# One segment of the modulation vector, computed by GpSimd during the mixers

## The chip, the cores and the metric

The kernel runs on one core of a Trainium2 chip. The core has TensorE (PE, matrix products into PSUM), VectorE (DVE), ScalarE (ACT), GpSimd (POOL) and SyncE (SP, which issues the weight loads here); all but SyncE's queue work on tiles in SBUF. The metric is the device time of one execution in microseconds (us); less is better.

## What is computed

Two transformer blocks on 256 tokens of width 2048, all in float32. The first block begins with a modulation vector of six segments of 2048 values from the condition `c`:

```python
c_act = jax.nn.silu(c)
mod = c_act @ ada_w[l] + ada_b[l]
sh1, sc1, g1, sh2, sc2, g2 = jnp.split(mod, 6, axis=-1)
h = rmsnorm(x, norm1_g[l]) * (1.0 + sc1[:, None]) + sh1[:, None]
x = x + g1[:, None] * token_mixer(h, ...)
h = rmsnorm(x, norm2_g[l]) * (1.0 + sc2[:, None]) + sh2[:, None]
x = x + g2[:, None] * moe_ffn(h, ...)
```

`ada_w` is 2048 x 12288. Segment 5 is `g2`, the factor behind the experts. `token_mixer` projects `h` to queries, keys and values, runs four kinds of attention (mixers) and projects their outputs with `w_out`. The second block (a long convolution, a gating unit, a feed-forward layer) takes no part of the modulation.

## The kernel before

A float32 product is made of three products of a split operand (`mm3`, L155): each weight tile that arrives in SBUF (`wraw`) is copied by ScalarE into a high part (`whi`, L146), VectorE takes the remainder (`wlo`, L149), and TensorE runs `hi*hi`, `lo*hi`, `hi*lo` (L158 to L160). There are five `wraw` buffers and three pairs of `whi` and `wlo`. One chunk is 256 rows by 512 columns of a weight, 512 KB.

The stages follow each other: `phase0` (the filters of the second block, segments 0 and 1 of the modulation, the first projections, to about 200 us), `mixers` (the other projections, the attentions and `w_out`, to about 620 us), the router, the experts (`moe`), then `block2`. All that the change touches runs in `mixers`.

A segment of the modulation is computed in four blocks of 512 columns, each in four steps (`ada_steps`, L456). A step loads two pieces of `ada_w`, 256 rows by 512 columns each (L467), so four row tiles of 128, and multiplies each row tile by its 128 values of `silu(c)`. There are two ways to do that. On TensorE (L473) four matmuls with 32 equal columns of `silu(c)` add up in one bank of PSUM; after the last step VectorE copies the bank to `arow` (L488), TensorE transposes it (L491), and VectorE sums the parts and adds the bias. On VectorE (`dve`) the first row tile is multiplied by its value of `silu(c)` per partition (L475), each other one is multiplied and added to `arow` in one instruction (L477), and at the end four matmuls with a column of ones sum over the partitions (L485). `ADA_DVE` lists the blocks that take the second way: blocks 1 and 3 of segments 2, 4, 3 and 5.

Steps of the segments run between other work: `rest` (L609) yields step by step in the order of segments 2, 4, 3, 5; every chunk of a projection adds 0.5 to an account and every softmax batch 0.7 (`hook`), and a step is written whenever the account reaches 1. What is left is written behind `w_out`. Pieces go to seven buffers in turn (`ada_place`: four named `a`, three `a2`); a load waits until its buffer has been read.

Every engine works in order through its own instructions. Their order is set by a scheduler in the framework, from the order in which the code is written, priorities and its own cost estimates, so an edit can move instructions on every engine. A softmax batch (`softmax_batch`) is a chain: TensorE's scores (L820), VectorE's sum with the bias (L837) and maximum (L839), ScalarE's exponential (L845), TensorE's transposes (L850), VectorE's copy (L852), TensorE's product with the values (L857). The mixers have 30 batches, 12 of them in the first attention stage (`nsa`), which also begins with a chain of small steps (L933 to L992).

Of the kernel before, what the change touches and what calls it, by code (L numbers as in the profile page):

```python
# [9 lines left out]
F32 = mybir.dt.float32  # L10
# [3 lines left out]
OP = mybir.AluOpType  # L14
# [4 lines left out]
P = 128  # L19
# [6 lines left out]
DFF = 5632  # L26
KF = DFF // P
HOOK_GEMM, HOOK_ATT = 0.5, 0.7
ADA_DVE = [(s, b) for s in (2,4,3,5) for b in (1,3)]

PAD = 16
TINY = float(np.finfo(np.float32).tiny)
# [107 lines left out]
class Body:  # L140
# [312 lines left out]
            return self.wp.tile([P, 2, 512], F32, name="wraw", tag="wraw", bufs=self.nraw)  # L453
        return self.piece([P, 2, 512], t)

    def ada_steps(self, seg, b, dve=False):  # L456


        nc, w = self.nc, self.i["ada_w"][0]
        c0 = seg * D + b * 512  # L460
        sb = self.awp.tile([P, 512], F32, name="arow", tag="arow", bufs=1)
        ps = None if dve else self.bank("ada")
        for q in range(4):
            for h in range(2):
                k0 = 4 * q + 2 * h
                raw = self.ada_place()
                self.last_ada = nc.sync.dma_start(raw, w[k0 * P:(k0 + 2) * P, c0:c0 + 512]  # L467
                                                  .rearrange("(k p) n -> p k n", p=P))
                for j in range(2):
                    k, r = k0 + j, raw[:, j]  # L470
                    if not dve:
                        m = 32 * (2 * h + j)
                        nc.tensor.matmul(ps[m:m + 32], self.cact[:, k], r, start=q == 0, stop=q == 3)  # L473
                    elif k == 0:
                        nc.vector.tensor_scalar(sb, r, self.cs[:, k:k + 1], None, OP.mult)  # L475
                    else:
                        nc.vector.scalar_tensor_tensor(sb, r, self.cs[:, k:k + 1], sb, OP.mult, OP.add)  # L477
            if q < 3:
                yield
        n = seg * 16 + b * 4  # L480
        bias, mod = self.v["ada_b"][:, n:n + 4], self.mod[:, seg, b * 4:b * 4 + 4]
        pt = self.bank("ada")
        if dve:
            for a in range(4):
                nc.tensor.matmul(pt[:, a:a + 1], sb[:, a * P:(a + 1) * P], self.ones[:, 0:1], start=True, stop=True)  # L485
            nc.vector.tensor_tensor(mod, pt[:, :4], bias, OP.add)
        else:
            nc.vector.tensor_copy(sb, ps)  # L488
            pt = pt.rearrange("p (a q) -> p a q", a=4)
            for a in range(4):  # L490
                nc.tensor.transpose(pt[:, a], sb[:, a * P:(a + 1) * P], self.ident)  # L491
            s = self.tmp.tile([P, 4], F32, name="adas", tag="modg", bufs=2)
            nc.vector.tensor_reduce(s, pt.rearrange("p a (j r) -> p a r j", r=32)[:, :, 0], AX.X, OP.add)
            nc.vector.tensor_tensor(mod, s, bias, OP.add)
        yield


    def bias_tables(self):
# [104 lines left out]
    def mixers(self):  # L603
        nc, tc, i = self.nc, self.tc, self.i
# [2 lines left out]
        xs = lambda k: (hh[:, k], hl[:, k])  # L607

        def rest():  # L609
            for seg in (2, 4, 3, 5):  # L610
                for b in range(4):
                    yield from self.ada_steps(seg, b, (seg, b) in ADA_DVE)
        bg, last = rest(), self.last_ada
        due = [0.0]

# [7 lines left out]
        with ExitStack() as c0:  # L623
# [9 lines left out]
            def project(col, tag, perm=False, mul=None):  # L633
                t = self.piece([P, 4, S], "k") if tag == "k" else qk(tag, tag)
                for m, p in enumerate(self.gemm(w, KD, col, 512, xs, C4, hook, perm)):
                    take(t[:, m], p, mul)
                return t
# [28 lines left out]
            q, k = project(0, "q", mul=scale), project(512, "k")  # L666
# [3 lines left out]
            q, k = project(2304, "q", mul=scale), project(2816, "k")  # L670
# [31 lines left out]
            acc = self.new_acc()  # L702
# [5 lines left out]
            for g in range(4):  # L708
# [4 lines left out]
                for m in range(4):  # L713
                    k = g * 4 + m
# [28 lines left out]
            r = v[:, 2:4]  # L743
# [5 lines left out]
            t = self.rt.tile([P, 2, 4], F32, name="gnorm")  # L749
# [891 lines left out]
```

## Time and profile before

| what | us |
|---|---|
| median of three runs (lowest, highest) | 2642.29 (2641.45, 2646.45) |
| the profiled execution | 2653.08 |
| its span | 2651.0 |

| engine | busy us | share of the span |
|---|---|---|
| TensorE, matmul | 2578.2 | 97% |
| TensorE, weight load | 2263.1 | 85% |
| VectorE | 1788.8 | 67% |
| ScalarE | 1333.8 | 50% |
| GpSimd | 7.2 | 0% |

All rows come from the profiled execution, which is 10.8 us above the median. Matmuls overlap, and the profile models their ends: a burst of them is priced by the distance between starts. Busy time of other engines is that of each instruction by itself. A row of waits names the engine that waited, its instruction, whom it waited for, then the total in us, how many times and the longest. PEclk is the granted clock of TensorE as a share of full speed (2.4 GHz), DMA the mean busy share of the 16 DMA engines, GB/s what they moved. "SPq" is SyncE's queue, which issues the loads.

### The profile page before, as it was taken

The numbers are of one execution on the slowest core, as the hardware profiler recorded it, in microseconds if no ns is written. First come the engines' busy times: TensorE is split into PE (matmuls) and PEld (weight loads), VectorE is DVE, ScalarE is ACT, GpSimd is POOL, SyncE is SP. The second block draws the span as 40 slices with busy tenths as digits, with TensorE's granted clock in tenths as the row PEclk, the third lists the DMA queues.
The fourth block names the chain that finished last, engine by engine and source line by source line (L and its number), as shares of the span: only waits on it lengthen the run. The fifth ranks groups of instructions, "written<-read, shape, count | busy, mean of one in ns | idle before, by whom it ended". The sixth has DMA issues, their size and how long they took to land.

```text
span 2651.0 us, 43628 instructions
## 1 busy us (share of the span) xinstructions
PE 2578.2 (97%) x17355; PEld 2263.1 (85%) x17355; DVE 1788.8 (67%) x2513; ACT 1333.8 (50%) x1774; POOL 7.2 (0%) x20
## 2 busy tenths in 40 slices
PE   6998999998999999999999999999999999999997
PEld 2476888888788878787998899999999999998886
DVE  4647777777889898988787655555655555555444
ACT  2333444545777777776444444444544444443443
POOL 0000000000000000000000000000000000000000
PEclk7998999998999999999999999999999999999999
DMA  9898799893899999997554555555555556556664
GB/s 358 288 299 292 258 328 323 301 311 115 297 334 326 330 334 376 344 367 281 176 167 128 182 184 184 188 185 186 184 188 190 187 189 190 187 189 199 191 195 138
DMA packets 320394, 640.81 MB, mean 242 GB/s; under 512 B 21748, under 2 KB 36116, under 8 KB 319416
## 3 DMA queue, kind: packets, MB, share of 16 engines
q1 hardware_dynamic: 310768, 618.83, 69.0%
q10 hardware_dynamic: 8392, 13.89, 1.6%
q0 software_dynamic: 1024, 5.25, 0.6%
q8 instruction: 137, 2.24, 0.3%
q14 instruction: 73, 0.60, 0.1%
HBM read 631.02 MB, written 6.35 MB: 240 GB/s over the span
## 4 chain that ended last, share of the span: by engine, by line
PE 72%; DVE 2%; ACT 1%; issue 1%; DMA 0%; ACTq 0%; DVEq 0%
PE ps_y L159 18%; PE ps_y L158 18%; PE ps_y L160 18%; PE ps_u L159 2%; PE ps_g L159 2%; PE ps_g L158 2%; PE ps_u L160 2%; PE ps_u L158 2%; PE ps_g L160 2%; DVE wlo L149 1%; PE ps_b L158 0%; PE ps_b L160 0%; PE ps_b L159 0%; DMA ws<-in_sgu_w_s_dram 0%; ACT whi L146 0%
## 5 line engine op out<-in xcount | busy, mean ns | idle before, releaser
L149 DVE TENSOR_TENSOR wlo<-wraw,whi 128x1024 fp32r<-128x1024 f32 (+1 forms) x972 | 1162.8, 1204 | 651.4 <-ACT whi L146 631.9
L146 ACT ACTIVATE whi<-wraw 128x1024 fp32r<-128x1024 f32 (+1 forms) x972 | 1011.1, 1044 | 933.5 <-PE ps_y L159 457.9
L158 PE MATMUL ps_y<-hH,whi 128*128 128x256 f32 x2432 | 681.5, 280 | 0.0
L160 PE MATMUL ps_y<-hH,wlo 128*128 128x256 f32 x2432 | 679.9, 280 | 0.0
L159 PE MATMUL ps_y<-hL,whi 128*128 128x256 f32 x2432 | 678.6, 279 | 0.0
L158 PEld LDWEIGHTS ps_y<-hH,whi 128*128 128x128 f32 x2432 | 456.8, 188 | 1.9 <-issue 1.7
L160 PEld LDWEIGHTS ps_y<-hH,wlo 128*128 128x128 f32 x2432 | 456.7, 188 | 1.7 <-issue 1.3
L159 PEld LDWEIGHTS ps_y<-hL,whi 128*128 128x128 f32 x2432 | 456.2, 188 | 1.8 <-issue 1.7
L158 PE MATMUL ps_mm<-hH,whi 128*128 128x256 f32 (+1 forms) x784 | 227.2, 290 | 4.4 <-ACT whi L146 4.4
L160 PE MATMUL ps_mm<-hH,wlo 128*128 128x256 f32 (+1 forms) x784 | 226.6, 291 | 2.1 <-DVE wlo L149 2.0
L159 PE MATMUL ps_mm<-hL,whi 128*128 128x256 f32 (+1 forms) x784 | 224.8, 287 | 0.0
L158 PEld LDWEIGHTS ps_mm<-hH,whi 128*128 128x128 f32 (+1 forms) x784 | 149.9, 191 | 25.1 <-issue 12.0
L160 PEld LDWEIGHTS ps_mm<-hH,wlo 128*128 128x128 f32 (+1 forms) x784 | 148.4, 190 | 10.7 <-DVE wlo L149 5.2
L159 PEld LDWEIGHTS ps_mm<-hL,whi 128*128 128x128 f32 (+1 forms) x784 | 148.4, 189 | 1.2 <-issue 0.6
L159 PE MATMUL ps_y<-wlo,actH 128*128 128x512 f32 x352 | 137.2, 390 | 0.0
L160 PE MATMUL ps_y<-whi,actL 128*128 128x512 f32 x352 | 137.1, 389 | 0.0
L158 PE MATMUL ps_y<-whi,actH 128*128 128x512 f32 x352 | 137.0, 390 | 0.0
L159 PE MATMUL ps_y<-wlo,piece 128*128 128x512 f32 x256 | 101.9, 398 | 0.2
L160 PE MATMUL ps_y<-whi,piece 128*128 128x512 f32 x256 | 100.5, 393 | 0.3 <-DVE piece L149 0.3
L158 PE MATMUL ps_y<-whi,piece 128*128 128x512 f32 x256 | 92.0, 394 | 0.7 <-ACT piece L146 0.7
L473 PE MATMUL ps_ada<-piece,cact 128*32 128x512 f32 x488 | 90.1, 655 | 2.5 <-DMA piece<-in_ada_w_dram 1.7
L477 DVE SCALAR_TENSOR_TENSOR arow<-piece,cs,arow 128x512 f32<-128x512 f32 x120 | 89.3, 744 | 1.9 <-DMA piece<-in_ada_w_dram 0.9
(521 smaller groups left out, 3898.5 us busy)
## 6 DMA issues: line engine op xcount, KB each, us to landing
wraw<-in_w_in_dram SPq DMA_DIRECT2D x224, 512.0 KB, 4.1
piece<-in_ada_w_dram SPq DMA_DIRECT2D x186, 512.0 KB, 6.8
wraw<-in_w_ffn_in_dram SPq DMA_DIRECT2D x176, 512.0 KB, 4.5
wraw<-in_exp_w_down_dram SPq DMA_DIRECT2D x125, 512.0 KB, 5.5
wraw<-in_exp_w_up_dram SPq DMA_DIRECT2D x124, 512.0 KB, 5.6
wraw<-in_exp_w_gate_dram SPq DMA_DIRECT2D x122, 512.0 KB, 5.4
wraw<-in_w_ffn_out_dram SPq DMA_DIRECT2D x88, 512.0 KB, 3.7
wraw<-in_w_out_dram SPq DMA_DIRECT2D x64, 512.0 KB, 4.9
```

What stands on the lines that cost most here:

```text
L146: self.nc.scalar.activation(dst, src, AF.Copy)
L149: self.nc.vector.tensor_tensor(dst, src, h.bitcast(F32), OP.subtract)
L158: mm(ps, a[0], b[0], start=start, stop=False)
L159: mm(ps, a[0], b[1], start=False, stop=False)
L160: mm(ps, a[1], b[0], start=False, stop=stop)
L473: nc.tensor.matmul(ps[m:m + 32], self.cact[:, k], r, start=q == 0, stop=q == 3)
L477: nc.vector.scalar_tensor_tensor(sb, r, self.cs[:, k:k + 1], sb, OP.mult, OP.add)
```

## The change

All four blocks of segment 5 go to GpSimd. GpSimd has no instruction in this kernel that multiplies and adds at once, so each row tile but a block's first is multiplied in place (the piece is written over) and then added to an accumulator of its own, `prow`: 64 products and 60 sums. The end of a block is that of the VectorE way, four matmuls with ones. The steps of segment 5 no longer come last: after every three steps of segments 2, 4 and 3 one of segment 5 is written, and the account counts it as a step, so there are 64 steps as before. Line numbers behind the edits rise by 1 to 16.

```diff
--- before.py
+++ after.py
@@ -26,7 +26,7 @@
 DFF = 5632
 KF = DFF // P
 HOOK_GEMM, HOOK_ATT = 0.5, 0.7
-ADA_DVE = [(s, b) for s in (2,4,3,5) for b in (1,3)]
+ADA_DVE = [(s, b) for s in (2, 4, 3) for b in (1, 3)]
 
 PAD = 16
 TINY = float(np.finfo(np.float32).tiny)
@@ -453,12 +453,13 @@
             return self.wp.tile([P, 2, 512], F32, name="wraw", tag="wraw", bufs=self.nraw)
         return self.piece([P, 2, 512], t)
 
-    def ada_steps(self, seg, b, dve=False):
+    def ada_steps(self, seg, b, dve=None):
 
 
         nc, w = self.nc, self.i["ada_w"][0]
         c0 = seg * D + b * 512
-        sb = self.awp.tile([P, 512], F32, name="arow", tag="arow", bufs=1)
+        tag = "prow" if dve is self.nc.gpsimd else "arow"
+        sb = self.awp.tile([P, 512], F32, name=tag, tag=tag, bufs=1)
         ps = None if dve else self.bank("ada")
         for q in range(4):
             for h in range(2):
@@ -472,9 +473,9 @@
                         m = 32 * (2 * h + j)
                         nc.tensor.matmul(ps[m:m + 32], self.cact[:, k], r, start=q == 0, stop=q == 3)
                     elif k == 0:
-                        nc.vector.tensor_scalar(sb, r, self.cs[:, k:k + 1], None, OP.mult)
+                        dve.tensor_scalar(sb, r, self.cs[:, k:k + 1], None, OP.mult)
                     else:
-                        nc.vector.scalar_tensor_tensor(sb, r, self.cs[:, k:k + 1], sb, OP.mult, OP.add)
+                        self.add_product(dve, sb, r, self.cs[:, k:k + 1])
             if q < 3:
                 yield
         n = seg * 16 + b * 4
@@ -493,6 +494,14 @@
             nc.vector.tensor_reduce(s, pt.rearrange("p a (j r) -> p a r j", r=32)[:, :, 0], AX.X, OP.add)
             nc.vector.tensor_tensor(mod, s, bias, OP.add)
         yield
+
+    def add_product(self, engine, acc, t, c):
+
+        if engine is self.nc.vector:
+            engine.scalar_tensor_tensor(acc, t, c, acc, OP.mult, OP.add)
+            return
+        engine.tensor_scalar(t, t, c, None, OP.mult)
+        engine.tensor_tensor(acc, acc, t, OP.add)
 
 
     def bias_tables(self):
@@ -607,9 +616,16 @@
         xs = lambda k: (hh[:, k], hl[:, k])
 
         def rest():
-            for seg in (2, 4, 3, 5):
-                for b in range(4):
-                    yield from self.ada_steps(seg, b, (seg, b) in ADA_DVE)
+
+            far = (x for b in range(4) for x in self.ada_steps(5, b, nc.gpsimd))
+            for n, _ in enumerate(x for seg in (2, 4, 3) for b in range(4)
+                                  for x in self.ada_steps(seg, b, nc.vector if (seg, b) in ADA_DVE else None)):
+                yield
+                if n % 3 == 2:
+                    next(far, None)
+                    yield
+            for _ in far:
+                yield
         bg, last = rest(), self.last_ada
         due = [0.0]
 
```

What the built program shows, at the three places that matter most. First GpSimd, in whose list nothing stood between the fills of the first attention stage (`cs`) and the load of the router's overflow count (`ovi`). Before:

```order
L294 MEMSET gap 128x8
L975 MEMSET cs 128x128 x2
L1333 TENSOR_LOAD ovi
L1334 COMPARE_AND_BRANCH
L1334 UNCONDITIONAL_BRANCH x2
```

Now:

```order
L294 MEMSET gap 128x8
L991 MEMSET cs 128x128 x2
L476 ISA
L476 TENSOR_SCALAR prow<-piece,cs 128x512
L503 TENSOR_SCALAR piece<-piece,cs 128x512
L504 TENSOR_TENSOR prow<-prow,piece 128x512
L503 TENSOR_SCALAR piece<-piece,cs 128x512 x2
L504 TENSOR_TENSOR prow<-prow,piece 128x512 x2
```

One block is one product into `prow` and then 15 pairs of a product and a sum; four such blocks stand in a row.

Second the queue of loads on SyncE, from the loads of the compression weights (`nsa_cmp`) at the start of the first attention stage. Before:

```order
L929 DMA wraw<-in_nsa_cmp_w_k_dram 128x8x128 x2
L929 DMA wraw<-in_nsa_cmp_w_v_dram 128x8x128 x2
L467 DMA piece<-in_ada_w_dram 128x2x512 x16
L191 DMA wraw<-in_w_in_dram 128x2x512
L467 DMA piece<-in_ada_w_dram 128x2x512 x2
```

Now:

```order
L945 DMA wraw<-in_nsa_cmp_w_k_dram 128x8x128 x2
L945 DMA wraw<-in_nsa_cmp_w_v_dram 128x8x128 x2
L468 DMA piece<-in_ada_w_dram 128x2x512 x9
L191 DMA wraw<-in_w_in_dram 128x2x512
L468 DMA piece<-in_ada_w_dram 128x2x512 x5
```

The next weight of a projection stood behind sixteen pieces and stands behind nine.

Third TensorE a little later, from the scores of the compressed keys (`kc`, `q`) to the first softmax batch. Before:

```order
L978 MATMUL ps_b<-kc,q 128x15 x8
L485 MATMUL ps_ada<-vec,arow 128x1 x4
L473 MATMUL ps_ada<-piece,cact 32x512 x5
L992 MATMUL ps_b<-vec,cs 128x128
L820 MATMUL ps_b<-piece,q 128x256 x4
L473 MATMUL ps_ada<-piece,cact 32x512 x9
L850 MATMUL ps_b<-vec,s 128x128 x4
```

Now:

```order
L994 MATMUL ps_b<-kc,q 128x15 x8
L158 MATMUL ps_mm<-hH,whi 128x256
L159 MATMUL ps_mm<-hL,whi 128x256
L158 MATMUL ps_mm<-hH,whi 128x256
L159 MATMUL ps_mm<-hL,whi 128x256
L160 MATMUL ps_mm<-hH,wlo 128x256
L158 MATMUL ps_mm<-hH,whi 128x256
L1008 MATMUL ps_b<-vec,cs 128x128
L836 MATMUL ps_b<-piece,q 128x256 x4
```

Ahead of the transpose of the compressed weights (L992, now L1008) stood nine matmuls of the modulation; now six plain products of the next projection stand there, and 18 more follow behind the scores.

## Rows read from the trace of the kernel before

**Rows 1.** The page: what the DMA queues moved by slice; the chain that ended last.
```profile
GB/s 358 288 299 292 258 328 323 301 311 115 297 334 326 330 334 376 344 367 281 176 167 128 182 184 184 188 185 186 184 188 190 187 189 190 187 189 199 191 195 138
...
PE 72%; DVE 2%; ACT 1%; issue 1%; DMA 0%; ACTq 0%; DVEq 0%
```

**Rows 2.** Busy time by stretch: start:end us, length, busy us (x instructions) by engine, clock, DMA.
```profile
200.00:300.00 100.00, 92.23 (x692) 73.35 (x691) 72.51 (x136) 37.71 (x88) 0.00 (x0) 0.88 0.75 267
300.00:400.00 100.00, 99.21 (x707) 82.14 (x706) 71.73 (x115) 47.20 (x93) 0.00 (x0) 1.00 0.92 319
400.00:500.00 100.00, 99.92 (x712) 82.97 (x710) 68.80 (x109) 46.75 (x89) 0.00 (x0) 1.00 0.90 306
500.00:600.00 100.00, 98.84 (x811) 90.44 (x807) 83.41 (x160) 48.58 (x93) 0.00 (x0) 1.00 0.92 320
```

**Rows 3.** Waits of TensorE, 200 to 590 us: who waited for whom, total us, times, longest.
```profile
PE ps_b L937 <- DVE four L935: 2.3, 2, 1.8
PE ps_ada L485 <- DVE arow L477: 2.1, 2, 1.8
PE ps_b L850 <- ACT s L845: 1.4, 3, 1.1
```

**Rows 4.** Timeline of TensorE, 308 us: start, length us, engine, instruction.
```profile
308.14 0.28 PE L160 MATMUL ps_mm<-hH,wlo 128*128 128x256 f32 x1
308.35 1.07 PE L473 MATMUL ps_ada<-piece,cact 128*32 128x512 f32 x8
309.35 0.38 PE L158 MATMUL ps_mm<-hH,whi 128*128 128x256 f32 x1
309.57 0.28 PE L159 MATMUL ps_mm<-hL,whi 128*128 128x256 f32 x1
```

**Rows 5.** The same view at 317 and at 577 us.
```profile
317.17 0.28 PE L159 MATMUL ps_mm<-hL,whi 128*128 128x256 f32 x1
317.29 0.60 PE L491 MATMUL ps_ada<-vec,arow 128*128 128x128 f32 x4
317.64 0.36 PE L160 MATMUL ps_mm<-hH,wlo 128*128 128x256 f32 x1
...
576.59 0.28 PE L158 MATMUL ps_mm<-hH,whi 128*128 128x256 f32 x1
576.77 1.02 PE L485 MATMUL ps_ada<-vec,arow 128*128 128x1 f32 x8
577.66 0.37 PE L159 MATMUL ps_mm<-hL,whi 128*128 128x256 f32 x1
```

**Rows 6.** VectorE by form, 200 to 590 us: shape, count, busy us, mean ns, idle before.
```profile
L149 DVE TENSOR_TENSOR wlo<-wraw,whi 128x1024 fp32r<-128x1024 f32 x77 | 93.6, 1219 | 31.7 <-ACT whi L146 28.3 <-PE ps_ada L473 3.2
L477 DVE SCALAR_TENSOR_TENSOR arow<-piece,cs,arow 128x512 f32<-128x512 f32 x120 | 89.3, 744 | 1.9 <-DMA piece<-in_ada_w_dram 0.9
...
L488 DVE COPY arow<-ps_ada 128x512 f32<-128x512 f32 x8 | 5.5, 690 | 11.7 <-PE ps_ada L473 11.7
...
L475 DVE TENSOR_SCALAR arow<-piece,cs 128x512 f32<-128x512 f32 x8 | 3.8, 478 | 0.1
```

**Rows 7.** ScalarE by form, 200 to 590 us.
```profile
L146 ACT ACTIVATE whi<-wraw 128x1024 fp32r<-128x1024 f32 x77 | 81.1, 1057 | 125.5 <-PE ps_mm L159 48.4 <-issue 45.2 <-PE ps_mm L160 19.5
```

**Rows 8.** GpSimd by form, whole span.
```profile
L975 POOL MEMSET cs<- 128x128 f32 x2 | 0.3, 204 | 142.8 <-DVE fK L593 142.8
L294 POOL MEMSET gap<- 128x8 f32 x2 | 0.2, 104 | 394.0 <-PE ps_y L160 393.8 <-POOLq L1629 0.3
```

**Rows 9.** Timeline of TensorE in the first attention stage.
```profile
221.66 3.62 PE L473 MATMUL ps_ada<-piece,cact 128*32 128x512 f32 x10 [0.25 <-DVE mod L486]
...
225.21 0.48 PE L992 MATMUL ps_b<-vec,cs 128*128 128x128 f32 x1
```

**Rows 10.** Waits of the DMA queue on SyncE, 200 to 600 us.
```profile
SPq L467 <- PE ps_ada L473: 81.5, 27, 9.0
SPq L467 <- DVE arow L477: 60.4, 34, 7.3
```

## Prediction

> **What bounds the kernel now.** Start with the chain of waits: 72% of the chain that ended last lies on TensorE and 2% on VectorE [rows 1], so time is won by taking work off TensorE or by closing its gaps. All that the change touches lies in the mixers, about 200 to 590 us, so read the busy time by stretch next. From 300 to 600 us TensorE is busy 99.2, 99.9 and 98.8 us of each 100 at a granted clock of 1.00, the 2.4 GHz level. From 200 to 300 us it is busy 92.2 us at a mean of 0.88 [rows 2]. Its idle time over these 400 us is 7.8 + 0.8 + 0.1 + 1.2 = 9.8 us. The list of its waits shows for whom: VectorE or ScalarE, a microsecond or two at a time [rows 3]. VectorE is busy 72.5, 71.7, 68.8 and 83.4 us of each 100 [rows 2], a second engine with a quarter of its time free. ScalarE's waits say how far the weights are split ahead: before the copies into `whi` it sat idle 48.4 + 19.5 us until TensorE had released a buffer [rows 7], so TensorE, not the split, sets the pace. GpSimd does nothing here (the column of x0) [rows 2].
>
> A busy TensorE hides what an instruction costs, since matmuls overlap. The price is the spacing of starts in the timeline. Plain 256-column products start 0.12 us apart. Around one burst of four segment matmuls (eight records) the starts are 308.14 and 309.35, then 309.57 [rows 4]: 1.21 - 0.12 = 1.09 us, and 0.10 us lost in the next, wider spacing. So 1.19 us a burst.
>
> **The change part by part.** Segment 5 (`g2`) has four blocks of 512 columns. Before, blocks 0 and 2 are on TensorE and 1 and 3 on VectorE.
> - TensorE loses two blocks of four bursts: 8 x 1.19 = 9.5 us. It loses their transposes: 317.17 to 317.64 less 0.12, and 0.10 for the next spacing, is 0.45 us [rows 5], twice 0.9. It gains two blocks of the other kind, four 1-column matmuls each: 576.59 to 577.66 less 0.12 plus 0.10 is 1.05 us [rows 5], twice 2.1. Net 9.5 + 0.9 - 2.1 = 8.3 us off the engine that sets the pace.
> - VectorE loses two blocks of one product and 15 product-sums: 2 x (0.478 + 15 x 0.744) = 23.3 us, and two copies of 0.690 us [rows 6]: 24.7 us. The loss is off the path, and worth nothing but room.
> - GpSimd gains 64 products and 60 sums of 128x512. No row has such an operation. The nearest are its own fills: 204 ns for 128 elements and 104 ns for 8 [rows 8], or 0.83 ns an element and 0.10 us fixed. One pass over 512 is then 0.5 us, which as a lower bound gives 124 x 0.5 = 62 us. The upper bound counts a pass for each operand, two for a product (0.95 us) and three for a sum (1.4 us): 145 us. I take the middle, 104 us or 0.84 us an operation, as nothing stands nearer either end. A step of four row tiles is 6.7 us (4 to 9), and 16 steps in 390 us come every 24 us, so GpSimd keeps up and its own time is covered.
> - The four row matmuls of a GpSimd block wait for its last sum, and behind them, in order, stand all matmuls. In the built program at least 78 plain products, 9 us, lie between that sum and them. With a step of 4 to 9 us I price this wait at 0; if that cover went, each would cost up to 9 us, 36 in all.
> - Loads: the same pieces and bytes, a quarter of them for GpSimd, from the same seven buffers. A step takes two, so a buffer comes round after 3.5 steps, at 6.1 us a step 21 us; GpSimd holds its pair for 9 us at most. SyncE's queue already waits 81.5 us for TensorE and 60.4 us for VectorE to free pieces [rows 10] without TensorE idling, so 0.
> - The order of the first attention stage moves. Before, sixteen pieces go ahead of the next weight, and ten records of segment matmuls stand from 221.66 us until the transpose at 225.21 [rows 9]: 3.6 us in a chain of small dependent steps. Now nine go ahead, and plain products stand there instead, which themselves wait for the weight tenth in the queue. That could win 3.6 us or lose as much; I take 0 and keep both ends.
> - Segments 2, 4 and 3 finish later. The last is needed by the router's shift after the last projection, and its row matmuls still stand ahead of 246 plain products of that projection: 0.
> - The hidden term: VectorE and GpSimd side by side. No run shows both at work. If they don't meet, it is 0. If VectorE is stretched in proportion to GpSimd's time, 104 of 390 us or 27%, TensorE's present 9.8 us of idle time, mostly waits for VectorE, grows by 2.6 us. The upper end is in the second rival.
>
> Sum: -8.3 + 2.6 = -5.7 us. The profiled execution took 2653.1 us (span 2651.0), so 2647.4; the median of the runs lies 10.8 us under it, so **2636.6 us**.
>
> The Trainium skill, "SBUF — State Buffer", section "SBUF: two separate sides", says more than proportion: VectorE and GpSimd share one pair of ports as an exclusive lock, and a VectorE operation with two SBUF inputs and a GpSimd operation fully block each other. No run here shows it so far. The remainder `wlo` and the product-sums are of that kind, so it speaks against this change. "GPSIMD Engine Reference", section 3.1, has 4497 ns for a sum of 2048; a quarter, 1.12 us, is an estimate that lies between my bounds, and 60 such sums would be 67 us.
>
> **The rivals.**
> *The gain is eaten.* Remainders alone are 93.6 us and the product-sums that stay three quarters of 89.3, 67 us [rows 6], so VectorE reads two tiles at a time for 160 us of 390, 41%. If each of 124 GpSimd operations then holds up such a one for its 0.84 us, VectorE loses 0.41 x 124 x 0.84 = 43 us. It has 103 us idle [rows 2] and gets 24.7 back, so in sum it fits; but some of it falls where TensorE waits for the softmax. If a sixth, 7 us, reaches TensorE, the change gives 1 us: 2641. For it: the chain of attention is short of cover already [rows 3]. Against it: the split runs ahead, up to three buffers [rows 7].
>
> *VectorE sets the pace, slower than before.* There are 30 softmax batches; in each, TensorE's transposes follow a sum, a maximum and an exponential, the first two in VectorE's line behind remainders and product-sums. If each batch has one GpSimd operation put in front of it, 30 x 0.84 = 25 us reach TensorE, less 8.3: +17 us, 2659. At 0.5 us a batch it is +7, 2649. It decides from 8.3 / 30 = 0.28 us a batch: above that the kernel is slower. For it: VectorE's 83.4 us of the last 100 [rows 2], and the first block's four GpSimd steps all lie in the first attention stage. Against it: only three of the batches' transposes show a wait now, 1.4 us together [rows 3]. The lock that "SBUF — State Buffer" in the Trainium skill describes would act just so.
>
> *The loads bound the mixers, nothing is won.* 306 to 320 GB/s [rows 2] must become 2% more. Other slices carry 376 [rows 1], so I give this little; 2642.
>
> **How the numbers follow.** A measurement of this kernel can tell about 0.2%, 5.3 us, from no change. My forecast has 0.43, since the 8.3 us are counted in rows and most of what could take them back has free time on VectorE to hide in; the gain eaten 0.28; VectorE setting the pace 0.23; the loads 0.06. The forecast ends just beyond that bound, the eaten gain and the loads end within it, the other rival above it: faster 0.43, same 0.34, slower 0.23. The low end is 8.3 us with no contention and the 3.6 of the order: 2642.3 - 11.9 = 2630.4, so 2630; the high end takes in the slower rival up to some 0.7 us a batch (30 x 0.7 - 8.3 = 12.7), 2655.
>
> **What would show it.** Right: TensorE has eight bursts fewer in the mixers, GpSimd about 104 us busy there at 0.7 to 1.2 us an operation, TensorE's idle time from 200 to 600 us under 13 us, and no wait of the row matmuls for GpSimd. The remainders' mean of 1219 ns and the product-sums' 744 ns [rows 6] tell contention: unchanged speaks for the forecast's 0, longer by a third or more for the rivals. The waits for the softmax (1.4 us now) grown to 10 us or more would be the slower rival; a new wait of TensorE for `prow` would prove the cover wrong; idle before the `whi` copies given to DMA would be the loads. Anything different behind 650 us, where TensorE's order is the same, would be none of my cases.

## The result, and the profile after

Beside each other, in four runs each, the kernel before took 2644.4 us (2641.5 to 2649.6) and the changed one 2686.8 us (2674.5 to 2690.3): 1.0153 times as long, 95% interval 1.0130 to 1.0176. **It is 40 us slower.** The forecast was a gain of 5.7 us, and the range ended at 2655. The profiled execution has a span of 2684.4 us.

Busy time by stretch, with the columns of [rows 2]:

```profile
200.00:300.00 100.00, 90.08 (x663) 72.61 (x661) 74.44 (x130) 38.16 (x96) 49.11 (x31) 0.86 0.77 267
300.00:400.00 100.00, 87.93 (x604) 74.99 (x603) 67.53 (x89) 41.65 (x77) 41.25 (x25) 0.97 0.80 274
400.00:500.00 100.00, 92.76 (x636) 75.05 (x634) 71.48 (x95) 41.75 (x79) 54.59 (x32) 0.97 0.87 301
500.00:600.00 100.00, 88.72 (x696) 79.60 (x695) 86.96 (x145) 47.56 (x97) 53.75 (x30) 0.97 0.77 260
```

TensorE's idle time in these 400 us has gone from 9.8 to 40.5 us, its clock from 300 us on from 1.00 to 0.97. VectorE does fewer instructions (x89 for x115 in the second stretch) and is as busy as before: the mean one takes longer. The loads from 300 us on have fallen from between 306 and 320 GB/s to between 260 and 301.

TensorE's waits, 200 to 640 us, to be read against [rows 3]:

```profile
PE ps_b L899 <- DVE ob L896: 9.2, 6, 3.0
PE ps_mm L158 <- ACT whi L146: 7.9, 3, 4.3
PE ps_ada L486 <- DVE arow L501: 6.0, 2, 4.3
PE ps_b L873 <- DVE pts L868: 5.8, 7, 1.9
...
PE ps_b L866 <- ACT s L861: 2.4, 3, 1.1
```

The waits of the attention (`ob`, `pts`, `s`) come to 17.4 us. In the kernel before it was 1.9 us: 1.4 for `s` [rows 3], 0.3 for `pts`, 0.2 for `ob`. So it is `pts` and `ob` that have grown. A wait for `prow` is not in the list.

GpSimd by form, 150 to 640 us (the operations that no row of before showed):

```profile
L503 POOL TENSOR_SCALAR piece<-piece,cs 128x512 f32<-128x512 f32 x60 | 114.5, 1919 | 158.2 <-DMA piece<-in_ada_w_dram 97.2 <-DVE xT L709 18.4 <-DVE arow L501 14.7
L504 POOL TENSOR_TENSOR prow<-prow,piece 128x512 f32<-128x512 f32 x60 | 90.9, 1515 | 2.5
L476 POOL TENSOR_SCALAR prow<-piece,cs 128x512 f32<-128x512 f32 x4 | 6.4, 1595 | 87.2 <-DMA piece<-in_ada_w_dram 76.8 <-PE ps_b L873 10.4
```

In all 212 us; a step of four row tiles takes 4 x (1.92 + 1.52) = 13.7 us. VectorE by form, 200 to 630 us, to be read against [rows 6]:

```profile
L149 DVE TENSOR_TENSOR wlo<-wraw,whi 128x1024 fp32r<-128x1024 f32 x80 | 107.7, 1347 | 46.6 <-ACT whi L146 46.2 <-PE ps_b L836 0.3
L501 DVE SCALAR_TENSOR_TENSOR arow<-piece,cs,arow 128x512 f32<-128x512 f32 x90 | 82.5, 917 | 2.8 <-DMA piece<-in_ada_w_dram 2.0
L868 DVE COPY pts<-ps_b 128x512 f32<-128x512 f32 x30 | 20.7, 689 | 25.8 <-PE ps_b L866 25.8
...
L896 DVE SCALAR_TENSOR_TENSOR ob<-ob,orr,mixg 128x512 f32<-128x512 f32 x8 | 8.2, 1027 | 0.1
```

The remainder has gone from 1219 to 1347 ns, the product-sum from 744 to 917. The last of these forms, in the kernel before (200 to 630 us):

```profile
L880 DVE SCALAR_TENSOR_TENSOR ob<-ob,orr,mixg 128x512 f32<-128x512 f32 x8 | 5.9, 744 | 0.0
```

The small remainder `hL`, 128x256, has gone from 416 to 739 ns. The copy `pts`, which reads PSUM, has kept its 689 ns; the maximum over `s`, which reads one tile in SBUF, took 675 ns before and takes 676 now. So the stretched operations are those with two inputs in SBUF, and of those with one the product of a tile with a factor (`arow<-piece,cs`, 478 ns before [rows 6], 712 now).

Last ScalarE's copies of the weights, 200 to 630 us [rows 7], and the waits of the queue of loads, 200 to 640 us [rows 10]:

```profile
L146 ACT ACTIVATE whi<-wraw 128x1024 fp32r<-128x1024 f32 x80 | 84.1, 1056 | 146.9 <-PE ps_mm L159 62.9 <-DMA wraw<-in_w_in_dram 36.5 <-PE ps_mm L160 23.8
```

```profile
SPq L468 <- POOL prow L504: 117.1, 25, 9.4
SPq L191 <- DVE wlo L149: 97.4, 46, 5.1
SPq L468 <- PE ps_ada L474: 46.1, 10, 8.7
```

The queue now waits 117 us for GpSimd to free pieces. Not all of that is new: its waits for the three engines that free pieces have gone from 81.5 + 60.4 = 141.9 us to 117.1 + 46.1 + 12.3 = 175.5 (12.3 for VectorE). Weights stand behind those loads, and ScalarE has 36.5 us of idle time that ended with the arrival of a weight of `w_in`; with those of `w_out` it is 43.2 us, where the kernel before had 8.4 (idle time before all copies into `whi`, 200 to 640 us). Three suspects, then: VectorE's stretched operations (B), the loads held by GpSimd (A), the new order (C).

### The profile page after: what moved, and what is told of

Its sections match the earlier page's. It is cut to its first block, busy times and chain, and to the rows that moved or that the text cites. A ratio compares the mean times of both kernels' runs of the same rounds, so it can differ in the third digit from the quotient of the medians.

```text
span 2684.4 us, 43631 instructions
## 1 busy us (share of the span) xinstructions
PE 2579.2 (96%) x17299; PEld 2270.6 (85%) x17299; DVE 1814.1 (68%) x2477; ACT 1333.4 (50%) x1774; POOL 217.8 (8%) x144
## 4 chain that ended last, share of the span: by engine, by line
PE 71%; DVE 2%; ACT 1%; issue 1%; DMA 0%; ACTq 0%; DVEq 0%
PE ps_y L159 18%; PE ps_y L158 18%; PE ps_y L160 18%; PE ps_u L159 2%; PE ps_g L159 2%; PE ps_g L158 2%; PE ps_u L160 2%; PE ps_u L158 2%; PE ps_g L160 2%; DVE wlo L149 1%; PE ps_b L160 0%; PE ps_b L158 0%; PE ps_b L159 0%; DMA ws<-in_sgu_w_s_dram 0%; ACT whi L146 0%
## 5 line engine op out<-in xcount | busy, mean ns | idle before, releaser
L149 DVE TENSOR_TENSOR wlo<-wraw,whi 128x1024 fp32r<-128x1024 f32 (+1 forms) x972 | 1178.7, 1220 | 664.1 <-ACT whi L146 647.2
L503 POOL TENSOR_SCALAR piece<-piece,cs 128x512 f32<-128x512 f32 x60 | 114.5, 1919 | 158.2 <-DMA piece<-in_ada_w_dram 97.2
L504 POOL TENSOR_TENSOR prow<-prow,piece 128x512 f32<-128x512 f32 x60 | 90.9, 1515 | 2.5
```

Source lines behind the costliest of these rows:

```text
L149: self.nc.vector.tensor_tensor(dst, src, h.bitcast(F32), OP.subtract)
L503: engine.tensor_scalar(t, t, c, None, OP.mult)
L504: engine.tensor_tensor(acc, acc, t, OP.add)
```

## The experiments

All runs, each against the runs of before on its chip (medians 2641.2 to 2644.6 us; 0.001 of the ratio is 2.6 us):

| kernel | us | ratio | 95% interval |
|---|---|---|---|
| changed kernel | 2686.8 | 1.0153 | 1.0130 to 1.0176 |
| new order, VectorE instead of GpSimd | 2659.3 | 1.0057 | 1.0037 to 1.0077 |
| changed, divided ring | 2668.9 | 1.0094 | 1.0069 to 1.0120 |
| new order, VectorE, divided ring | 2648.7 | 1.0024 | 1.0009 to 1.0039 |
| new order, VectorE, GpSimd beside (own loads) | 2688.3 | 1.0164 | 1.0137 to 1.0190 |
| old order, new split, VectorE | 2643.8 | 1.0008 | 0.9993 to 1.0022 |
| new order, old split | 2670.3 | 1.0097 | 1.0075 to 1.0119 |
| new order, VectorE, GpSimd beside | 2686.3 | 1.0165 | 1.0143 to 1.0188 |
| old order, twelve blocks on VectorE | 2653.1 | 1.0029 | 1.0015 to 1.0043 |
| late order, VectorE | 2645.4 | 1.0006 | 0.9989 to 1.0022 |
| late order, VectorE, divided ring | 2642.3 | 0.9995 | 0.9978 to 1.0012 |
| late order, GpSimd, divided ring | 2678.5 | 1.0120 | 1.0082 to 1.0158 |
| new order, VectorE, GpSimd's products beside | 2659.5 | 1.0062 | 1.0037 to 1.0086 |
| old order, two blocks off TensorE, given to nobody | 2639.0 | 0.9986 | 0.9974 to 0.9997 |
| new order, VectorE, GpSimd's sums beside | 2671.3 | 1.0109 | 1.0092 to 1.0126 |

### GpSimd out, the order kept

```diff
-            far = (x for b in range(4) for x in self.ada_steps(5, b, nc.gpsimd))
+            far = (x for b in range(4) for x in self.ada_steps(5, b, nc.vector))
```

(`prow` stays an accumulator of its own.)

> The order of the change (a step of segment 5 behind every three others, its own accumulator), but VectorE computes all of segment 5 and GpSimd nothing. Beside 2644 us before and 2687 us changed. Theory A (the loads: GpSimd frees its pieces late, SyncE's queue stands still and the weights behind it come late): about 2636 to 2645, since VectorE frees a piece in 1.5 us. Theory B (the ports: VectorE's operations and with them the softmax chain are held up by GpSimd): the same, 2636 to 2645. Theory C (the new order alone costs it): about 2680, GpSimd or not.

Measured 1.0057, between the expected times: 15 us of the 40 are there without GpSimd, and 25 come with it (1.0153 less 1.0057). The remainder is back at 1219 ns, the product-sums at 744.

### The ring divided, with GpSimd and without

```diff
-        turn = "aabakbawkab" if self.first else "aababab"
+        turn = "aabakbawkab" if self.first else "b" if far else "a"
```

(`far` is true for segment 5, whose pieces then go round three buffers, the others' round four.)

> The change, but the seven buffers are divided: segment 5 has the three named a2 for itself, the other segments the four named a, so that no load of another segment waits for GpSimd; segment 5's next load comes four steps later. Theory A: most of the 42 us goes, about 2650 (some remains, as the other segments run ahead less far). Theory B: about 2680 or more, since GpSimd and VectorE meet as before. Theory C: about 2680.

> The control of the divided buffers: VectorE computes segment 5, with the order of the change and the divided buffers. All theories but C: within 8 us of the kernel with the order alone; what it lies above that is the price of four buffers for the other segments in place of seven.

With GpSimd the divided ring takes off 1.0153 - 1.0094, 16 us (each interval is about 6 us wide to either side). The queue's wait for GpSimd falls from 117.1 us in 25 waits to 12.1 in 3, and the idle time before the `whi` copies that ended with a weight's arrival from 43.2 us to 17.5 (19.6 in the new order with VectorE). So GpSimd did make weights late. But with VectorE in GpSimd's place the same ring gives 9 us, where I had expected a price and no gain, so about half is no matter of GpSimd's. The other half, 7 us, the intervals can't tell from nothing (-4 to 18). And between the two runs with divided rings 0.0070, 18 us, still stand (intervals: 11 to 26). That is what GpSimd costs where it holds up hardly a load (A nearly taken out).

### GpSimd beside, with no work of the kernel's

```diff
+                if seg == 5:
+                    self.beside(h, raw)
...
+    def beside(self, h, raw):
+        g = self.nc.gpsimd
...
+        t = self.side
+        for j in range(2):
+            c = raw[:, 0, 0:1] if h == j == 0 else self.cs[:, j:j + 1]
+            g.tensor_scalar(t, t, c, None, OP.mult)
+            g.tensor_tensor(t, t, t, OP.add)
```

The first form of this took `c` from a small load of its own, on the queue of loads:

> The order of the change with VectorE computing segment 5 from its pieces, and beside it GpSimd running as many products and sums of 128x512 on a tile of its own whose result nobody reads; it holds no piece. One tiny load a step, which GpSimd's first product of the step reads, paces it. Theory A: the time of the kernel with the order alone, within 8 us. Theory B: 30 to 45 us above it, and VectorE's remainders and product-sums as long as in the changed kernel (1347 and 917 ns) or longer.

It gave 1.0164, but the queue's waits showed one of 24.2 us in 5 for that small tile, so part of it could be the loads. The second form takes the factor from the piece itself:

> The changed order with VectorE computing segment 5, and beside it GpSimd with 64 products and 64 sums on a tile of its own, as in the earlier run of that kind, but without that run's small loads on the queue of loads: the first product of each step takes its factor from a column of the piece that has just landed, so GpSimd holds one piece of each step for one product and nothing else that the loads need. B, the ports (GpSimd's passes stretch VectorE's with two inputs in SBUF): 2659 + 20 to 29 = 2679 to 2688 us with the remainder at 1300 ns or more and the product-sum above 850. A, the loads: 2659 to 2664 us, and the earlier run's extra came from its own small loads.

1.0165, the same: 0.0108, 28 us, over the run without GpSimd, in which all else is written alike. So 128 passes of GpSimd that nobody waits for cost as much as the whole step from VectorE to GpSimd in the changed kernel. It is not the same sum inside, though: there VectorE has 64 passes fewer and the loads are held; here neither.

The waits of TensorE (200 to 640 us) show a part of the way from VectorE to TensorE. The run without GpSimd has 1.8 us for `pts` and no wait for `ob`; with GpSimd beside it is

```profile
PE ps_b L914 <- DVE ob L911: 8.7, 6, 2.3
PE ps_b L888 <- DVE pts L883: 5.8, 6, 1.6
```

The wait for the exponential `s` is 4.4 us in both. So 13 us of new waiting stand in the chain of attention, in a run whose queue of loads has no wait for GpSimd in its list. In all TensorE's idle time from 200 to 600 us goes from 19.6 to 43.4 us.

### Products alone, sums alone

The last `tensor_tensor` left out, and then instead the products (but for the first of each step, over 8 columns):

> The run with GpSimd's 64 products and 64 sums beside VectorE (2686 us), with the 64 products alone: the sums of the tile with itself are left out. The run without GpSimd stood at 2659 us. If only GpSimd's passes with two tensors hold VectorE up: 2657 to 2663 us, and a product falls to its undisturbed time. If every pass does, in proportion to its time: 27 x 118 / 193 = 16 us, about 2676 us. If the products do it alone: 2683 us or more.

> The run with GpSimd's 64 products and 64 sums beside VectorE (2686 us) with the 64 sums alone; of the products only the first of each step is left, over 8 columns, so that GpSimd still starts with the landed piece. The run with the products alone stood at 2659 us, as the one with no GpSimd. If the sums do it alone: 2680 to 2690 us, with VectorE's remainder at 1270 ns or more. If it takes both side by side: 2659 to 2667 us.

The forms of interest, 200 to 680 us, with the products alone:

```profile
L149 DVE TENSOR_TENSOR wlo<-wraw,whi 128x1024 fp32r<-128x1024 f32 x92 | 112.6, 1226 | 36.6 <-ACT whi L146 30.8 <-DMA piece<-in_ada_w_dram 4.4 <-PE ps_ada L477 1.0
L515 DVE SCALAR_TENSOR_TENSOR arow<-piece,cs,arow 128x512 f32<-128x512 f32 x90 | 71.4, 794 | 0.4
L515 DVE SCALAR_TENSOR_TENSOR prow<-piece,cs,prow 128x512 f32<-128x512 f32 x57 | 44.3, 778 | 12.5 <-DMA piece<-in_ada_w_dram 12.4
...
L510 POOL TENSOR_SCALAR side<-side,cs 128x512 f32<-128x512 f32 x45 | 88.6, 1968 | 4.2
L510 POOL TENSOR_SCALAR side<-side,piece 128x512 f32<-128x512 f32 x15 | 29.0, 1931 | 263.9 <-DMA piece<-in_ada_w_dram 263.9
```

with the sums alone:

```profile
L149 DVE TENSOR_TENSOR wlo<-wraw,whi 128x1024 fp32r<-128x1024 f32 x89 | 116.5, 1312 | 31.1 <-ACT whi L146 24.2 <-DMA piece<-in_ada_w_dram 4.4 <-PE ps_mm L160 1.2
L517 DVE SCALAR_TENSOR_TENSOR arow<-piece,cs,arow 128x512 f32<-128x512 f32 x90 | 71.4, 793 | 0.4
L517 DVE SCALAR_TENSOR_TENSOR prow<-piece,cs,prow 128x512 f32<-128x512 f32 x57 | 46.2, 810 | 9.7 <-DMA piece<-in_ada_w_dram 9.4
L512 POOL TENSOR_TENSOR side<-side 128x512 f32<-128x512 f32 x60 | 80.6, 1343 | 4.8
```

and with both:

```profile
L149 DVE TENSOR_TENSOR wlo<-wraw,whi 128x1024 fp32r<-128x1024 f32 x85 | 109.8, 1295 | 34.7 <-ACT whi L146 32.0 <-DMA piece<-in_ada_w_dram 1.6 <-PE ps_ada L477 1.0
L516 DVE SCALAR_TENSOR_TENSOR arow<-piece,cs,arow 128x512 f32<-128x512 f32 x90 | 77.2, 858 | 0.4
L516 DVE SCALAR_TENSOR_TENSOR prow<-piece,cs,prow 128x512 f32<-128x512 f32 x57 | 53.0, 930 | 9.7 <-DMA piece<-in_ada_w_dram 9.6
...
L511 POOL TENSOR_TENSOR side<-side 128x512 f32<-128x512 f32 x60 | 74.8, 1246 | 5.0
```

Over the run without GpSimd the times are +1, +14 and +28 us. Add up, for these three forms of VectorE, the count times what each has gained over 1219, 744 and 745 ns: 7, 16 and 27 us. Over all forms of VectorE it is 11, 26 and 42 us. The time grows with the stretch, and so do the waits for `pts` and `ob` together: 3.0, 7.1 and 14.5 us, 1.8 without GpSimd. The products' 118 us of GpSimd cost next to nothing; there GpSimd mostly gives way: its product took 1968 ns in the mean and 1564 at the least. One that began 0.19 us ahead of the remainder at 260.68 us took 2.76 us, and the remainder its usual 1.22. The sums' 81 us stretch VectorE. Neither expectation fits whole: the sums do not do it alone, and why both together cost twice the sums is not shown.

A mean hides how the stretch comes about. The product-sum's shortest, median and longest duration (view of the tile `arow`, 200 to 630 us), before:

```profile
L477 DVE SCALAR_TENSOR_TENSOR arow<-piece,cs,arow x120: 698/744/753, 201.6 to 575.9; 128x512 f32<-128x512 f32 x120
```

in the changed kernel, and beside the products alone:

```profile
L501 DVE SCALAR_TENSOR_TENSOR arow<-piece,cs,arow x90: 734/752/1792, 209.4 to 598.2; 128x512 f32<-128x512 f32 x90
```

```profile
L515 DVE SCALAR_TENSOR_TENSOR arow<-piece,cs,arow x90: 698/744/1174, 204.2 to 577.1; 128x512 f32<-128x512 f32 x90
```

The median has hardly moved, and the timelines say why: 47 of the 90 in the changed kernel meet no operation of GpSimd, and these take 753 ns at most. Of those that meet one, some stand still for up to 1.04 us beside sums and products, 0.43 us beside products. One of each kind, GpSimd's operation and the product-sum that began inside it, in the changed kernel and beside the products alone:

```profile
363.45 1.76 POOL L504 TENSOR_TENSOR prow<-prow,piece 128x512 f32<-128x512 f32 x1
364.15 1.61 DVE L501 SCALAR_TENSOR_TENSOR arow<-piece,cs,arow 128x512 f32<-128x512 f32 x1
```

```profile
440.15 1.67 POOL L510 TENSOR_SCALAR side<-side,cs 128x512 f32<-128x512 f32 x1
440.31 1.17 DVE L515 SCALAR_TENSOR_TENSOR arow<-piece,cs,arow 128x512 f32<-128x512 f32 x1
```

The first ends 0.55 us behind the sum, and so do the two others that met a sum alone, at 299.97 and 444.85 us, though they began at other points of it. The second ends 0.34 us ahead of the product's end. It is no sharing of a rate but a wait of one for the other: to the end of a sum, but not to the end of a product.

### The order, apart from the split

Old order with the new split (a list of the kernel before changed), and new order with the old split (TensorE and VectorE eight blocks each):

```diff
-ADA_DVE = [(s, b) for s in (2,4,3,5) for b in (1,3)]
+ADA_DVE = [(s, b) for s in (2, 4, 3) for b in (1, 3)] + [(5, b) for b in range(4)]
```

```diff
-ADA_DVE = [(s, b) for s in (2, 4, 3) for b in (1, 3)]
+ADA_DVE = [(2, 1), (4, 1), (4, 3), (3, 1)]
```

> The kernel before with one list of its changed: all four blocks of segment 5 on VectorE (ten blocks there, six on TensorE), the order of the work, the loads and the rings as before, no GpSimd. With the run in the changed order that had the same ten blocks on VectorE (2659.3 us) it tells apart the two things that may have cost that run 18 us. C, the order (eight loads fewer put ahead of the next weight, segment 5 strewn among the others): this run has the old order, so it shows the relief alone, 2641 - 8 = about 2633 us, at most 2641, and the changed order then costs about 20 to 26 us. D, VectorE's load (two more blocks of 16 products at 744 ns, 24 us): this run is as late as that one, 2655 to 2662 us, with VectorE above 80% in the stretches from 200 to 600 us and the waits of TensorE there for VectorE's tiles grown.

> The changed order alone, at the old split: TensorE and VectorE have eight blocks each as in the kernel before, VectorE all four of segment 5 (in an accumulator of their own) and four of the others, TensorE the other eight; no GpSimd. C, the order costs: 2641 + 18 to 26 = 2659 to 2667 us, with TensorE's idle time from 200 to 600 us above 20 us. D, VectorE's load was what cost: 2641 us, within 5.

0.0008 and 0.0097: the split alone costs nothing that can be measured, the order alone 26 us, and both together (the run without GpSimd) 15 us. D falls: VectorE can take the two blocks; the order is what it costs. The two are not a plain sum: in the new order the step of two blocks from TensorE to VectorE gains 11 us (3 to 18), in the old order it gives 2 us of loss (-2 to 6). Why is open.

Where? TensorE from 220 to 240 us in the new order at the old split:

```profile
220.00:240.00 20.00, 14.78 (x57) 10.69 (x57) 14.75 (x27) 5.48 (x18) 0.00 (x0) 0.50 0.77 249
```

in the kernel before:

```profile
220.00:240.00 20.00, 19.39 (x111) 10.86 (x111) 11.12 (x24) 6.46 (x20) 0.00 (x0) 0.83 0.86 302
```

and in the changed kernel:

```profile
220.00:240.00 20.00, 15.88 (x83) 11.67 (x79) 16.95 (x27) 6.16 (x18) 12.97 (x10) 0.76 0.70 254
```

In the new order without GpSimd the clock is 0.50, the 1.2 GHz level, and half the matmuls get done. In the 20 us ahead it is 0.82 (before 0.74), in the 20 us behind 0.74 (before 1.00). In the changed kernel, where plain products stand behind the scores, it is 0.76. The timeline of TensorE there, first in the new order, then before:

```profile
219.87 0.44 PE L1008 MATMUL ps_b<-vec,cs 128*128 128x128 f32 x1 [3.14 <-DVE cs L1003]
220.25 2.08 PE L836 MATMUL ps_b<-piece,q 64*128 64x256 f32 x8
224.99 1.18 PE L866 MATMUL ps_b<-vec,s 128*128 128x128 f32 x4 [2.66 <-ACT s L861]
226.95 1.97 PE L873 MATMUL ps_b<-piece,pts 128*128 128x64 f32 x8 [0.78 <-DVE pts L868]
```

```profile
225.62 1.72 PE L820 MATMUL ps_b<-piece,q 64*128 64x256 f32 x8
227.27 2.76 PE L473 MATMUL ps_ada<-piece,cact 128*32 128x512 f32 x18
230.00 0.93 PE L850 MATMUL ps_b<-vec,s 128*128 128x128 f32 x4
230.87 1.05 PE L473 MATMUL ps_ada<-piece,cact 128*32 128x512 f32 x4
231.85 1.10 PE L857 MATMUL ps_b<-piece,pts 128*128 128x64 f32 x8
```

In the kernel before, 32 records of the modulation's matmuls (those of [rows 9] and the two rows here) lie where TensorE waits in the new order: for `cs`, the exponential and the copy. In the new order the next such records come behind this chain, from 247.7 us on; TensorE waits 3.1 + 2.7 + 0.8 us, and eight products with the values take 1.97 us instead of 1.10.

### The first stage left in the old order

```diff
-                if n % 3 == 2:
+                if n >= 12 and n % 2:
```

Segment 5 begins only behind the first twelve steps (by this condition behind the fourteenth), and then has every third step (every fourth in the change). The second run also divides the ring from then on, the third has GpSimd compute segment 5 as the change does.

> The changed order with VectorE computing segment 5 (as the run of that kind at 2659.3 us), but its first step is written only behind the twelfth step of the others, so that the first attention stage stands in the order of the kernel before: 32 matmuls of the modulation among the softmax batches, sixteen pieces ahead of the next weight. E, the first stage costs (TensorE has no fillers there, waits, and runs at a lower clock): about 10 us less, 2645 to 2653, with a granted clock from 200 to 300 us of 0.88 or more in place of 0.81. A, the rest is the shared ring's: then not below 2655 us.

> The same with the ring divided as soon as segment 5 has begun (its pieces in three buffers, the others in four). If the first stage and the shared ring are together all that the order costs, this run stands where the kernel with the new split in the old order stood: 2638 to 2646 us. If strewing the steps costs something by itself, 2650 us or more.

> The same again with GpSimd computing segment 5, as the change does: the order's cost taken out, GpSimd kept. B, the ports: 20 to 27 us above the run with VectorE in its place, 2660 to 2670 us, with VectorE's remainder at 1300 ns or more. If GpSimd's cost came from the order and the ring (A, C), it is within 5 us of that run.

With VectorE 1.0006: 13 us less than the same kernel with the first stage in the new order, and the first stretch is back. In the new order with VectorE TensorE was busy 89.7 us of it, at a clock of 0.81; now:

```profile
200.00:300.00 100.00, 94.25 (x709) 77.65 (x710) 77.98 (x145) 39.56 (x97) 0.00 (x0) 0.91 0.83 283
```

So the first stage is nearly the whole cost of the order at the new split. The divided ring gives 3 us more (0.9995), which the intervals can't tell from nothing, where it had given 9 before: the two gains overlap, and with the first stage whole the shared ring costs little. With GpSimd 1.0120, 33 us over its twin with VectorE (22 to 44): without the order's cost and with divided rings the change still loses. Its remainders took 1371 ns, as B had it, but the time is above B's 2670 us. That this run is no better than the divided ring in the new order (1.0094) I had not expected; its runs spread from 2665.8 to 2694.6, segment 5's steps follow each other more closely in it, and the cause stays open.

### What the relief of TensorE is worth

```diff
+                        m = 8 if seg == 5 and b in (0, 2) else 512
-                        nc.vector.scalar_tensor_tensor(sb, r, self.cs[:, k:k + 1], sb, OP.mult, OP.add)
+                        nc.vector.scalar_tensor_tensor(sb[:, :m], r[:, :m], self.cs[:, k:k + 1], sb[:, :m], OP.mult, OP.add)
```

(`ADA_DVE` as in the run of the old order with the new split. The rest of these two blocks' sums is left out.)

> The kernel before, in its own order, with blocks 0 and 2 of segment 5 taken off TensorE and given to nobody: VectorE makes their first product over all 512 columns and the other 15 product-sums over 8 columns only, so that every piece is still loaded, read and freed in the same order. What it leaves out is the rest of those two blocks' sums. TensorE loses eight bursts, VectorE does 2 x 15 small instructions more. The relief counted in the prediction: 8.3 us less, 2633 to 2636 us beside a run of before at 2641 to 2644. If TensorE's bursts there were covered by something else that bounds (the loads, the chain of the softmax): within 2 us of before. The run with the two blocks whole on VectorE stood 2 us over before; the difference to it is then what 30 product-sums of 744 ns on VectorE cost.

0.9986, a gain of 3.7 us (0.8 to 6.9): there, but about half of the 8.3. One place took some back: from 470 to 505 us TensorE waits 3.3 us for a copy into `whi` and 2.9 us for the remainder `wlo` of a weight, waits that the kernel before did not have. ScalarE and VectorE first make twelve tiles `hH` and `hL` there, 3.8 and 4.1 us in a row, and so the split of the weight ends last. And with the two blocks whole on VectorE (0.0008) 30 product-sums, 22 us of work, had cost 6 us (1 to 11 by the intervals). The last run has four more blocks on VectorE than before:

> The kernel before with three of the four blocks of each segment on VectorE (twelve there, four on TensorE), the order as before. Under C (VectorE has room, TensorE bounds): four bursts fewer at about 1.2 us for each of four steps are worth up to 4 x 4 x 1.2 = 19 us less on TensorE by the bursts and their row matmuls given back, so about 2625 to 2637 us. Under D (VectorE has no room): 48 us more on VectorE, 2660 to 2680 us.

1.0029, 8 us slower, between C and D: of VectorE's 103 idle us, some 47 (four blocks of 0.478 + 15 x 0.744) cannot be had for nothing, though TensorE has four blocks less.

No kernel here beats the one before by more than the 0.2% that can be told; the nearest with all of the computation is 0.9995.

## Why the prediction was wrong

- **TensorE bounds the mixers: right, but only just.** The 8.3 us are worth 3.7 when nothing else is changed; in the new order the same relief, paid for on VectorE, gave 11.
- **"The hidden term: VectorE and GpSimd side by side", 2.6 us: this step failed.** GpSimd in VectorE's place cost 25 us at the new order, 18 with divided rings. I had taken a stretch in proportion and applied it to TensorE's waits alone. Beside sums 26 us of stretch on VectorE cost 14 us of time, beside sums and products 42 cost 28. In the changed kernel the remainders are 80 x 128 ns = 10 us longer, the product-sums 90 x 173 ns = 16, all forms together 46 us (each form's count times what its mean has gained over the run without GpSimd). My own rival had 43 us of loss on VectorE, near enough though from an operation half as long as measured, and let a sixth of it reach TensorE. My sign for contention, a third or more on the mean, was set too high: the means rose by 10 and 23%. Planned work on VectorE is cheaper than that (22 us of it cost 6): it stands where the order has room, while a stop by GpSimd meets whatever is running, the chain to the softmax too. The waits show the chain (`ob`, `pts`, `s`: 1.9 to 17.4 us; in the run beside `ob` and `pts` from 1.8 to 14.5), but that this makes the difference to planned work is argued, not tried. The slower rival had the right chain but not the wait in it: TensorE's wait for the exponential went from 1.4 to 2.4 us only. That its 25 us for GpSimd is what GpSimd cost is luck, as it goes by 0.84 us an operation; and its 2659 us lay above the range, which ended at 2655.
- **The Trainium skill's rule** ("SBUF — State Buffer", section "SBUF: two separate sides": an exclusive lock, held for a whole instruction, not a split of bandwidth). The traces agree that it is a wait and no split: product-sums that began at three different points of a sum all ended 0.55 us behind it. They don't agree on the whole instruction: beside products of 1.56 us and more, no product-sum was over 0.43 us late, and the one shown ended 0.34 us ahead of its product.
- **GpSimd's 0.84 us an operation: mis-sized.** 1.92 and 1.52 us measured, 212 us in all, over my upper bound of 145. Fills of a few elements were no guide to a pass over 512. "GPSIMD Engine Reference" of the Trainium skill, section 3.1, from which I had estimated 1.12 us for a sum, was nearer: 1.26 us at the least, 1.52 in the mean.
- **Loads, 0: failed by the same mis-sized operation.** A step is 13.7 us, not "9 us at most", so with the ring coming round in 21 us the pieces were late: 117 us of the queue's waits, weights late at ScalarE. The divided ring got back 16 us of the 40, 9 of which it also gets back without GpSimd; whether the other 7 are more than noise is not shown.
- **The order of the first stage, 0 with ends of 3.6 us: failed.** At the new split with VectorE it cost about 13 us. I had priced the piece of the chain ahead of the transpose; the modulation's matmuls further down, among the softmax batches, were the fillers, and without them the clock fell to half. In the changed kernel it fell to 0.76 there, so what the first stage costs with GpSimd at work is not shown.
- **The row matmuls' wait, 0: right.** No wait of TensorE for `prow`. GpSimd kept up with the step of 24 us. Behind the mixers nearly nothing but the shift of the whole shows: in the profiled executions the first product into `ps_u`, behind the router, starts 31 us later than before (698.7 for 668.0), the last one 33 us later (2431.6 for 2398.3).

The parts, in the order in which the runs take them apart: new split with VectorE +2 us, the new order +13, GpSimd in VectorE's place +25, sum 40. They hold for this path alone: with the first stage in the old order and divided rings, GpSimd in VectorE's place cost 33 us (22 to 44).

## What to carry to other kernels

GpSimd's idle time is not free time: sums of two tensors in SBUF stop VectorE's operations of that kind, so measure such a pass beside the kernel first, on a tile that nobody reads, with the engine that did the work left at it. Where small pieces of independent work are moved, look at what they were filling: a burst in the middle of a dependent chain can be worth more than its own length, and the clock besides. And price a ring of buffers by the whole step of its slowest reader.

## What the runs showed of the hardware

- GpSimd's product of one 128x512 tensor with a factor per partition took 1556 ns at the least (1655 median), its sum of two such tensors 1257 (1388): the operation with fewer tensors is the slower one. On the tile of its own: 1562 for the product, 1037 for the sum of the tile with itself.
- Some of VectorE's smallest operations are stretched most in proportion. Two rows of the changed kernel, 128x1 each, where the kernel before had 153 and 151 ns:

```profile
L268 DVE TENSOR_TENSOR orr<-orr 128x1 f32<-128x1 f32 x8 | 3.1, 391 | 0.2
L265 DVE TENSOR_TENSOR orr<-orr 128x1 f32<-128x1 f32 x8 | 2.6, 330 | 0.2
```

They stand in the chain ahead of `ob`, for which TensorE waits longest now.
